# Hymba block, one Trainium2 core: the Gram blocks of the first chunk cut to half width and put first, a smaller first transfer, a final scaling without GpSimd, and a recurrence that begins four matmuls later

## The chip, the cores and the metric

The kernel runs on one core of a Trainium2 chip. The metric is the device time of one execution in microseconds; the median of three runs stands for a kernel. TensorE is called PE here, VectorE DVE, ScalarE ACT, GpSimd POOL and SyncE SP, as in the profile.

## The reference

One layer. A sequence of 512 tokens of width 2048, with 16 learned meta tokens ahead of it, is normalised, projected, sent through a recurrent branch (16 heads of 64, in pairs: 8 pairs) and a gated convolution, mixed, added back and normalised.

```python
hn = _rmsnorm(h_res, norm_in_g[l])                 # (1, 528, 2048)
P  = hn @ w_in[l]                                  # 8 pieces of 1024 columns and a low-rank piece of 128
Pr = Pr + (prev - Pr) * mu_shift[l]                # token shift of r, k, v, g_r and the low-rank columns
decay = exp(-exp(w_raw)); a = sigmoid(a0 + al @ a_lora_up); kk = normalised(k * k_k)
k = k * (1.0 + (a - 1.0) * k_a[l])
# per head, state S of 64x64, over time:
S = S * w_t - (S kk_t) (kk_t*a_t)^T + v_t k_t^T;   y_t = S r_t
y_a = (groupnorm(y) + bonus) * silu(g_r)
y_b = Bg * causal_conv3(Cg * hc) * silu(g_c)
out = _rmsnorm(h_res + concat(y_a, y_b) @ w_out[l], norm_f_g)[:, 16:]
```

## The kernel before

**Projection.** The whole input lies in SBUF as `xh` + `xl`, two parts that add up to the fp32 value, and the weights are split in the same way by `split_w` (L132 to L135, on ACT with DVE or POOL). Each projection therefore takes three matmuls per 128x128 block, hi·hi, hi·lo and lo·hi (`steps`, matmul at L328). `mains` is a generator: it yields one matmul at a time with an estimate of its time, 0.43 ns a column. The projections run in the order of a list `plan`, each into one or two PSUM banks of the pool `pm` with the tag "main"; `scaled` (L352) takes the finished result out of PSUM on DVE.

**Everything else is woven between projection matmuls.** A stage such as `prepare(i)` for head pair i issues its own instructions and then calls `fill(ns)`, which takes as many projection matmuls from `mains` as fill `ns` nanoseconds by the estimate. The table `FW` holds those amounts. So PE's instruction order is written out when the program is built, and a stage on PE always stands between projection matmuls. DVE and ACT are ordered by the scheduler of the tile framework, with `ahead()` (L583) as a raised priority; in some stretches `manual_schedule` keeps the written order.

**Gram blocks.** The sequence is cut into chunks: chunk 0 is the 16 meta tokens in a frame of 64 columns, chunks 1 to 8 hold 64 tokens each (`NCH` is 9). In `prepare(i)` the inner function `gram` (L680) multiplies for each chunk and each of the two heads a 64x128 stationary block of `bk` with a 64x128 moving block of `ar`, in fp32, that is two passes for each matmul. The moving block's first 64 columns are keys, its last 64 columns the receptances `r`; for chunk 0 the latter are zeros. The results go to `za` (chunks 0 to 3, two banks of the tag "tz"), `zc` (chunks 4 to 7, a bank of "misc" and one of "ser") and `ze` (chunk 8, two banks of "main", the tag of the projections). `masked` (L689, instruction at L692) copies them on DVE through the causal mask `gmask` into `gt`, which later transfers read. After the Gram stage `fill(FW["gram2"] ...)` puts projection matmuls, then come the norms `n2` (L714, L715) into "misc" and "tz" and the sum `zb` (L717) into "ser". A bank is written again only when its reader is done, so `za`, `zc` and `ze` each have somebody on PE waiting for their masks.

**Recurrence.** Inverses of the Gram blocks are made for two pairs at a time (`invert`); after the last two, `fill(FW["begin"])` (L929) puts projection matmuls ahead of the recurrence. `load_chunk` brings the operands of a chunk back from DRAM as `ct`, one transfer for each pair; `recur` starts with the matmuls `rz` (L958), four of them for each pair.

**Start.** PE warms up on four passes of a zero tile (`pwarm`, L187). Meanwhile four transfers bring `front`, an array packed by the host: the first (`bt`, 672 columns) has the gain, the first weight block and all 528 columns of `x` tile 0; the second (`r0`, 384 columns) three more weight blocks. `split_x` makes `xh` and `xl` of a tile, and the first projection matmuls (L495, into `ps_lora`) run over both halves of the columns with each operand pair before the next operand pair.

**End.** `finish_last` (L1416) scales the last 128 rows of the output in four pieces of 512 columns by the final norm's factor `r`, on DVE, ACT, POOL and DVE (L1419, L1421, L1423, L1424), and sends each piece off on SP's or ACT's queue.

Of the kernel before, what the change touches and what calls it, by code (L numbers as in the profile page):

```python
# [9 lines left out]
F32 = mybir.dt.float32  # L10
# [34 lines left out]
    tr=3200, lev=3000, cp=4200, out=1500, begin=19500, p=2900, u=2900, s=4800, last=3700, mix=2600,  # L45
# [32 lines left out]
def hymba_kernel(ctx: ExitStack, tc: tile.TileContext, xt, xtok, front, w_in, w_out, pv, lup, cst, msk, gf, out):  # L78
# [126 lines left out]
    def split_x(kt, cols=slice(0, L)):  # L205
        gain = ng[:, kt : kt + 1]
        nc.scalar.activation(xh[:, kt, cols], raw[kt][:, cols], AF.Copy, scale=gain)
        return nc.vector.scalar_tensor_tensor(
            out=xl[:, kt, cols], in0=raw[kt][:, cols], scalar=gain, in1=xh[:, kt, cols].bitcast(F32),
            op0=ALU.mult, op1=ALU.subtract,  # L210
        ).ins

    def square_x(kt, first=False):
        sq = accd if first else tr(f"sqx{kt}")[:, 0:L]
        nc.scalar.activation(sq, raw[kt], AF.Square)
        if not first:
            nc.vector.tensor_tensor(out=accd, in0=accd, in1=sq, op=ALU.add)
# [15 lines left out]
    F0, F1, F2 = KT + P + L, 4 * P + L, 8 * P + 2 * L  # L233
    fr = [view("bt", F0), view("r0", 3 * P), view("bk", F1), view("gt0", F2)]
# [5 lines left out]
    raw[0], raw[1] = fr[0][:, KT + P : F0], fr[2][:, 4 * P : F1]  # L240
# [10 lines left out]
    with tc.manual_schedule(engines={mybir.EngineType.DVE, mybir.EngineType.Activation}):  # L251
        split_piece(0, 0, fr[0][:, KT : KT + P])
        split_x(0, slice(0, L // 2))
        split_x(0, slice(L // 2, L))
        for n in (1, 2, 3):
            split_piece(n, 0, fr[1][:, (n - 1) * P : n * P])
        split_x(1)
        for n in range(4):
            split_piece(n, P, fr[2][:, n * P : (n + 1) * P])
        for kt in (2, 3):  # L260
            split_x(kt)
            if kt == 2:
                for n in range(4):
                    split_piece(n, 2 * P, fr[3][:, 2 * n * P : 2 * (n + 1) * P])
        split_w(1, later_w[0], nc.vector)
        for kt in range(4, 8):
            split_x(kt)
        split_w(3, later_w[1], nc.vector)
        square_x(2, True)
        square_x(3)  # L270
        for n in (2, 3):
            split_w(2 * n + 1, later_w[n], nc.vector)
        square_x(0)
        square_x(1)
        head = split_x(8)
# [207 lines left out]
    def mains():  # L483
# [5 lines left out]
        for k in range(4):  # L489
            for n, (ps, rg) in enumerate(four):  # L490
                if k == n == 0:
                    hi, lo = quarters[0]
                    for ww, xx, first in ((hi, xh, True), (lo, xh, False), (hi, xl, False)):
                        for p, (a, b) in zip(ps, rg):
# [132 lines left out]
    def prepare(i):  # L627
# [51 lines left out]
        gt = cq.tile([P, 2, NCH, P], F32, tag=f"gt{p}", name=f"gt{i}")  # L679
        def gram(z, c, c0):  # L680
            for h, hs, ho in heads:
# [3 lines left out]
                    ar[hs, c].rearrange("p a s -> p (a s)"),  # L685
# [3 lines left out]
        def masked(z, c0, c1):  # L689
            with ahead():  # L690
                for h in range(2):
                    nc.vector.tensor_tensor(  # L692
                        out=gt[:, h, c0:c1],
                        in0=z[h],
                        in1=gmask[:, h].unsqueeze(1).to_broadcast([P, c1 - c0, P]),
# [6 lines left out]
        ze = [pm.tile([P, 1, P], F32, tag="main", name=f"g{i}_8_{h}") for h in range(2)]  # L702
        for c in range(NCH):
            gram((za, zc, ze)[c // 4], c, c // 4 * 4)
        masked(za, 0, 4)
        masked(zc, 4, 8)
        masked(ze, 8, 9)
# [708 lines left out]
    def finish_last(t):  # L1416
# [6 lines left out]
        nc.gpsimd.tensor_scalar(out=here(t, 3), in0=here(t, 3), scalar1=r, scalar2=1.0, op0=ALU.mult, op1=ALU.mult)  # L1423
        nc.vector.tensor_scalar(out=here(t, 1), in0=here(t, 1), scalar1=r, scalar2=1.0, op0=ALU.mult, op1=ALU.mult)  # L1424
        nc.sync.dma_start(o[:, 512:1024], here(t, 1))
        nc.scalar.dma_start(o[:, 1536:DM], here(t, 3))
# [100 lines left out]
```

## Time and profile before

| | us |
|---|---|
| median of the runs | 1001.87 |
| lowest and highest of three runs | 1001.54, 1002.07 |
| the profiled execution's own time | 999.8 |
| its span in the trace | 997.9 |
| PE busy (share of the span) | 986.4 (99%) |
| DVE, ACT, POOL busy | 691.5, 412.7, 268.2 |

The granted clock of the profiled execution is 0.997. PE's busy time is a union of modelled intervals: a matmul's entry begins when its pass begins and ends later than the next one begins, so the distance between two starts is a better measure of what a matmul takes than its own duration. "PEld" is the loading of the stationary operand. A row of the timeline gives the start, the time covered, the engine, the line of the kernel, the instruction, the tile written and the tiles read, how many instructions the row joins, and in brackets the idle time before it with what ended that.

### The profile page before, as it was taken

The page shows a single profiled execution, that of the slowest core. Times are in us where ns is not written, and L with a number is a line of the kernel's source. Part 1 is how long each engine was busy: PE and PEld are TensorE (multiplying, and loading weights), DVE is VectorE, ACT ScalarE, POOL GpSimd, SP SyncE. Part 2 cuts the span into 40 slices and gives each one's busy share as a digit, 9 for nine tenths or more (in the row PEclk, how much of TensorE's full clock was granted, in tenths as well). Part 3 has the DMA queues.
Part 4 walks back from the last instruction along what each step waited for, and adds up shares of the span by engine and source line. Part 5 has one row for each costly group of instructions (what it writes and reads, how often), then busy time and mean ns, then how long its engine had stood idle before and what let it go on. Part 6 is the DMA issues. An engine that isn't in the chain of part 4 may idle for free.

```text
span 997.9 us, 22790 instructions
## 1 busy us (share of the span) xinstructions
PE 986.4 (99%) x9211; PEld 911.0 (91%) x9211; DVE 691.5 (69%) x1314; ACT 412.7 (41%) x770; POOL 268.2 (27%) x286
## 2 busy tenths in 40 slices
PE   9999999999999999999999999999999999999996
PEld 8999999999998999998999998989889898888885
DVE  7687975487765679735579735246555598999895
ACT  7554432353422534232534323233333325645553
POOL 0123323234322324222324222223242422011001
PEclk9999999999999999999999999999999999999998
DMA  9527485437683465854264854988783698698644
GB/s 337 155 70 198 112 218 150 115 105 179 149 226 108 107 178 128 221 148 118 84 180 119 224 142 125 355 259 281 219 262 94 195 260 229 212 297 218 143 102 168
DMA packets 184986, 179.48 MB, mean 180 GB/s; under 512 B 112177, under 2 KB 141617, under 8 KB 184369
## 3 DMA queue, kind: packets, MB, share of 16 engines
q1 hardware_dynamic: 182288, 169.12, 57.9%
q0 software_dynamic: 2304, 8.39, 4.9%
q8 instruction: 72, 1.18, 0.5%
q10 hardware_dynamic: 288, 0.52, 0.1%
q14 instruction: 34, 0.27, 0.1%
HBM read 139.28 MB, written 38.71 MB: 178 GB/s over the span
## 4 chain that ended last, share of the span: by engine, by line
PE 96%; DVE 1%; DMA 1%; issue 1%; POOL 0%; ACT 0%; DVEq 0%; POOLq 0%
PE ps_r L328 9%; PE ps_h L328 9%; PE ps_g L328 9%; PE ps_gc L328 9%; PE ps_B L328 9%; PE ps_v L328 9%; PE ps_C L328 8%; PE ps_k L328 8%; PE M L1243 8%; PE P L1243 4%; PE Q L1243 2%; PE g L682 2%; DMA ct<-opd 1%; PE ps_lora L328 1%; PE rz L958 1%; PE zs L1005 1%
## 5 line engine op out<-in xcount | busy, mean ns | idle before, releaser
L134 ACT CAST w<-wr 128x512 fp32r<-128x512 f32 x252 | 153.4, 619 | 281.0 <-PE ps_h L328 44.7
L135 POOL TENSOR_TENSOR w<-wr,w 128x512 fp32r<-128x512 f32 x119 | 165.8, 1395 | 371.5 <-ACT w L134 331.6
L135 DVE TENSOR_TENSOR w<-wr,w 128x512 fp32r<-128x512 f32 x133 | 99.2, 751 | 99.8 <-ACT w L134 99.6
L328 PE MATMUL ps_r<-xh,w 128*128 128x256 f32 (+1 forms) x512 | 95.2, 282 | 1.0 <-DVE gt L692 1.0
L328 PE MATMUL ps_k<-xh,w 128*128 128x256 f32 (+1 forms) x512 | 95.4, 284 | 0.0
L328 PE MATMUL ps_v<-xh,w 128*128 128x272 f32 (+1 forms) x512 | 95.4, 284 | 0.0
L328 PE MATMUL ps_h<-xh,w 128*128 128x258 f32 (+1 forms) x512 | 93.4, 282 | 0.0
L328 PE MATMUL ps_C<-xh,w 128*128 128x258 f32 (+1 forms) x512 | 93.2, 281 | 0.0
L328 PE MATMUL ps_g<-xh,w 128*128 128x258 f32 (+1 forms) x512 | 91.7, 280 | 0.0
L328 PE MATMUL ps_B<-xh,w 128*128 128x512 f32 x256 | 83.1, 394 | 0.0
L328 PEld LDWEIGHTS ps_r<-xh,w 128*128 128x128 f32 x512 | 80.2, 189 | 1.6 <-DVE gt L692 1.2
L328 PE MATMUL ps_gc<-xh,w 128*128 128x512 f32 x256 | 81.7, 393 | 0.0
L328 PEld LDWEIGHTS ps_k<-xh,w 128*128 128x128 f32 x512 | 80.3, 189 | 0.3
L328 PEld LDWEIGHTS ps_v<-xh,w 128*128 128x128 f32 x512 | 80.1, 189 | 0.3
L328 PEld LDWEIGHTS ps_C<-xh,w 128*128 128x128 f32 x512 | 79.6, 189 | 0.6
L328 PEld LDWEIGHTS ps_h<-xh,w 128*128 128x128 f32 x512 | 79.2, 189 | 0.7
L328 PEld LDWEIGHTS ps_g<-xh,w 128*128 128x128 f32 x512 | 79.2, 189 | 0.2
L328 PE MATMUL ps_k<-xl,w 128*128 128x256 f32 (+1 forms) x256 | 73.0, 285 | 0.0
L328 PE MATMUL ps_v<-xl,w 128*128 128x256 f32 (+1 forms) x256 | 72.5, 283 | 0.0
L328 PE MATMUL ps_g<-xl,w 128*128 128x256 f32 (+1 forms) x256 | 72.4, 283 | 0.0
L328 PE MATMUL ps_r<-xl,w 128*128 128x256 f32 (+1 forms) x256 | 72.1, 282 | 0.0
L328 PE MATMUL ps_C<-xl,w 128*128 128x256 f32 (+1 forms) x256 | 71.9, 281 | 0.0
(312 smaller groups left out, 2205.8 us busy)
## 6 DMA issues: line engine op xcount, KB each, us to landing
wr<-in_w_in_dram SPq DMA_DIRECT2D x126, 512.0 KB
ct<-opd SPq DMA_DIRECT2D x56, 320.0 KB
wo<-in_w_out_dram SPq DMA_DIRECT2D x21, 512.0 KB
opd<-gt SPq DMA_DIRECT2D x16, 576.0 KB
x<-in_w_out_dram POOLq DMA_DIRECT2D x16, 512.0 KB, 5.7
opd<-ar SPq DMA_DIRECT2D x8, 576.0 KB
opd<-bt SPq DMA_DIRECT2D x64, 64.0 KB
ct<-opd SPq DMA_DIRECT2D x16, 256.0 KB
```

Of the source, the lines that this page charges most:

```text
L134: nc.scalar.copy(hi, rq)
L135: low[q] = eng.tensor_tensor(out=lo, in0=rq, in1=hi.bitcast(F32), op=ALU.subtract).ins
L328: nc.tensor.matmul(ps[r], ww[:, w], xx[:, kt, a:b], start=(kt == 0 and n == 0), stop=(kt == KT - 1 and n == 2))
L682: nc.tensor.matmul(z[h][:, c - c0], bk[hs, c, h : h + 2, :].rearrange("p a s -> p (a s)"), ar[hs, c].rearrange("p a s -> p (a s)"), start= ...
L958: nc.tensor.matmul(z[e][ho if e else hs, 0, k], ct[e][hs, k, o : o + CH], uv(e, k, hs, h) if part else st[hs, 4 * e + k], start=(part == 0 ...
L1005: nc.tensor.matmul(zs[hs, j], bb[:, h], uv(e, k, everything, h), start=True, stop=True)
L1243: nc.tensor.matmul(bank[s], left(prod, jj, m, s), w, start=(jj == 0 and n == 0), stop=(jj == 7 and n == 2))
```

## The change

Four edits that have nothing to do with each other.

1. `gram` takes only the first 64 columns of `ar` as moving operand where the chunk is 0. Chunk 0 now goes to `ze`, which shrinks to 64 columns and is computed first and masked first; `za` holds chunks 1 to 4 and `zc` chunks 5 to 8. The upper half of `gt` for chunk 0 is now set to zero by a POOL memset.
2. The first transfer holds only the first 256 columns of `x` tile 0 (400 columns in all) and goes to `r0`; the other 272 go with the second transfer (656 columns) to `bt`. The first weight block's high part is made on DVE, not on ACT. The first matmuls finish the first half of the columns before the second half.
3. `finish_last` gives the piece that POOL scaled to DVE (192 columns) and ACT (320 columns).
4. `FW["begin"]` goes from 19500 to 19900.

```diff
@@ -42,7 +42,7 @@
 
 FW = dict(
     evac=34, start=1062, lora=2200, gram=8000, gram_b=13500, gram2=5500, misc=2000, v=2000, vt=1000, solve=24500, solve_first=30000,
-    tr=3200, lev=3000, cp=4200, out=1500, begin=19500, p=2900, u=2900, s=4800, last=3700, mix=2600,
+    tr=3200, lev=3000, cp=4200, out=1500, begin=19900, p=2900, u=2900, s=4800, last=3700, mix=2600,
 )
 
 
@@ -202,17 +202,17 @@
         for k in range(n):
             raw[a + k] = t[:, k * L : (k + 1) * L]
 
-    def split_x(kt, cols=slice(0, L)):
-        gain = ng[:, kt : kt + 1]
-        nc.scalar.activation(xh[:, kt, cols], raw[kt][:, cols], AF.Copy, scale=gain)
+    def split_x(kt):
+        gain, h = ng[:, kt : kt + 1], xh[:, kt, 0:L]
+        nc.scalar.activation(h, raw[kt], AF.Copy, scale=gain)
         return nc.vector.scalar_tensor_tensor(
-            out=xl[:, kt, cols], in0=raw[kt][:, cols], scalar=gain, in1=xh[:, kt, cols].bitcast(F32),
-            op0=ALU.mult, op1=ALU.subtract,
+            out=xl[:, kt, 0:L], in0=raw[kt], scalar=gain, in1=h.bitcast(F32), op0=ALU.mult, op1=ALU.subtract
         ).ins
 
     def square_x(kt, first=False):
         sq = accd if first else tr(f"sqx{kt}")[:, 0:L]
-        nc.scalar.activation(sq, raw[kt], AF.Square)
+        for cols, t in ((slice(0, L), raw[kt]),) if kt else x0:
+            nc.scalar.activation(sq[:, cols], t, AF.Square)
         if not first:
             nc.vector.tensor_tensor(out=accd, in0=accd, in1=sq, op=ALU.add)
 
@@ -230,14 +230,16 @@
 
     for n in range(4):
         quarters[2 * n] = slot_of(2 * n)
-    F0, F1, F2 = KT + P + L, 4 * P + L, 8 * P + 2 * L
-    fr = [view("bt", F0), view("r0", 3 * P), view("bk", F1), view("gt0", F2)]
+    X0 = L - SEQ // 2
+    F0, F1, F2 = KT + P + SEQ // 2, 4 * P + L, 8 * P + 2 * L
+    fr = [view("r0", F0), view("bt", X0 + 3 * P), view("bk", F1), view("gt0", F2)]
     o = 0
     for t in fr:
         nc.sync.dma_start(t, front[:, o : o + t.shape[1]])
         o += t.shape[1]
     ng = fr[0]
-    raw[0], raw[1] = fr[0][:, KT + P : F0], fr[2][:, 4 * P : F1]
+    x0 = ((slice(0, SEQ // 2), fr[0][:, KT + P : F0]), (slice(SEQ // 2, L), fr[1][:, 0:X0]))
+    raw[1] = fr[2][:, 4 * P : F1]
     for k in range(2):
         raw[2 + k] = fr[3][:, 8 * P + k * L : 8 * P + (k + 1) * L]
     later_w = [load_w(0, "g")]
@@ -249,11 +251,18 @@
     load_x("vs", 11, 1)
     nc.sync.dma_start(pvt, pv)
     with tc.manual_schedule(engines={mybir.EngineType.DVE, mybir.EngineType.Activation}):
-        split_piece(0, 0, fr[0][:, KT : KT + P])
-        split_x(0, slice(0, L // 2))
-        split_x(0, slice(L // 2, L))
+        hi, lo = (t[:, 0:P] for t in quarters[0])
+        w0 = fr[0][:, KT : KT + P]
+        nc.vector.tensor_copy(hi, w0)
+        nc.vector.tensor_tensor(out=lo, in0=w0, in1=hi.bitcast(F32), op=ALU.subtract)
+        for cols, t in x0:
+            nc.scalar.activation(xh[:, 0, cols], t, AF.Copy, scale=ng[:, 0:1])
+            nc.vector.scalar_tensor_tensor(
+                out=xl[:, 0, cols], in0=t, scalar=ng[:, 0:1], in1=xh[:, 0, cols].bitcast(F32),
+                op0=ALU.mult, op1=ALU.subtract,
+            )
         for n in (1, 2, 3):
-            split_piece(n, 0, fr[1][:, (n - 1) * P : n * P])
+            split_piece(n, 0, fr[1][:, X0 + (n - 1) * P : X0 + n * P])
         split_x(1)
         for n in range(4):
             split_piece(n, P, fr[2][:, n * P : (n + 1) * P])
@@ -490,8 +499,8 @@
             for n, (ps, rg) in enumerate(four):
                 if k == n == 0:
                     hi, lo = quarters[0]
-                    for ww, xx, first in ((hi, xh, True), (lo, xh, False), (hi, xl, False)):
-                        for p, (a, b) in zip(ps, rg):
+                    for p, (a, b) in zip(ps, rg):
+                        for ww, xx, first in ((hi, xh, True), (lo, xh, False), (hi, xl, False)):
                             nc.tensor.matmul(p, ww[:, 0:P], xx[:, 0, a:b], start=first, stop=False)
                             yield (b - a) * 0.43
                     continue
@@ -677,34 +686,37 @@
         fill(FW["gram_b" if p else "gram"] + shift)
 
         gt = cq.tile([P, 2, NCH, P], F32, tag=f"gt{p}", name=f"gt{i}")
+        nc.gpsimd.memset(gt[:, :, 0, CH:P], 0.0)
+
         def gram(z, c, c0):
             for h, hs, ho in heads:
                 nc.tensor.matmul(
                     z[h][:, c - c0],
                     bk[hs, c, h : h + 2, :].rearrange("p a s -> p (a s)"),
-                    ar[hs, c].rearrange("p a s -> p (a s)"),
+                    ar[hs, c].rearrange("p a s -> p (a s)") if c else ar[hs, c, 0],
                     start=True, stop=True,
                 )
 
-        def masked(z, c0, c1):
+        def masked(z, c0, c1, n=P):
             with ahead():
                 for h in range(2):
                     nc.vector.tensor_tensor(
-                        out=gt[:, h, c0:c1],
+                        out=gt[:, h, c0:c1, 0:n],
                         in0=z[h],
-                        in1=gmask[:, h].unsqueeze(1).to_broadcast([P, c1 - c0, P]),
+                        in1=gmask[:, h, 0:n].unsqueeze(1).to_broadcast([P, c1 - c0, n]),
                         op=ALU.mult,
                     )
 
 
         za = [pz.tile([P, 4, P], F32, tag="tz", name=f"g{i}_0_{h}") for h in range(2)]
         zc = [pi.tile([P, 4, P], F32, tag=("misc", "ser")[h], name=f"g{i}_4_{h}") for h in range(2)]
-        ze = [pm.tile([P, 1, P], F32, tag="main", name=f"g{i}_8_{h}") for h in range(2)]
-        for c in range(NCH):
-            gram((za, zc, ze)[c // 4], c, c // 4 * 4)
-        masked(za, 0, 4)
-        masked(zc, 4, 8)
-        masked(ze, 8, 9)
+        ze = [pm.tile([P, 1, CH], F32, tag="main", name=f"g{i}_8_{h}") for h in range(2)]
+        gram(ze, 0, 0)
+        for c in range(1, NCH):
+            gram((za, zc)[c // 5], c, 1 + c // 5 * 4)
+        masked(ze, 0, 1, CH)
+        masked(za, 1, 5)
+        masked(zc, 5, 9)
         fill(FW["gram2"] - shift + 1300 * (i == 1) + 2000 * (i == 3))
 
         n2 = tr(f"n2{i}")
@@ -1420,9 +1432,11 @@
         nc.sync.dma_start(o[:, 1024:1536], here(t, 2))
         nc.scalar.activation(here(t, 0), here(t, 0), AF.Copy, scale=r)
         nc.scalar.dma_start(o[:, 0:512], here(t, 0))
-        nc.gpsimd.tensor_scalar(out=here(t, 3), in0=here(t, 3), scalar1=r, scalar2=1.0, op0=ALU.mult, op1=ALU.mult)
         nc.vector.tensor_scalar(out=here(t, 1), in0=here(t, 1), scalar1=r, scalar2=1.0, op0=ALU.mult, op1=ALU.mult)
         nc.sync.dma_start(o[:, 512:1024], here(t, 1))
+        a, b = here(t, 3)[:, 0:192], here(t, 3)[:, 192:512]
+        nc.scalar.activation(b, b, AF.Copy, scale=r)
+        nc.vector.tensor_scalar(out=a, in0=a, scalar1=r, scalar2=1.0, op0=ALU.mult, op1=ALU.mult)
         nc.scalar.dma_start(o[:, 1536:DM], here(t, 3))
 
     with tc.manual_schedule(engines={mybir.EngineType.DVE, mybir.EngineType.Activation, mybir.EngineType.Pool}):
```

Line numbers move by 9 to 14 from L328 on: L328 becomes L337, L352 becomes L361, L682 becomes L693, L692 becomes L703, L958 becomes L970.

Three places of the instruction order follow. The first is PE at the Gram stage of pair 0, in the first stretch of projections: `ps_r_0` is a projection matmul, `g_0`, `g_4` and `g_8` are the banks `za`, `zc` and `ze`, with the head as the next number. Before:

```order
L328 MATMUL ps_r_0_1098<-xh,w_826 128x256
L682 MATMUL g_0_0_1136<-ar_755,bk_756 128x128
L682 MATMUL g_0_1_1137<-ar_755,bk_756 128x128
L682 MATMUL g_0_0_1136<-ar_755,bk_756 128x128
L682 MATMUL g_0_1_1137<-ar_755,bk_756 128x128
...
L682 MATMUL g_4_0_1138<-ar_755,bk_756 128x128
L682 MATMUL g_4_1_1139<-ar_755,bk_756 128x128
L682 MATMUL g_8_0_1140<-ar_755,bk_756 128x128
L682 MATMUL g_8_1_1141<-ar_755,bk_756 128x128
L328 MATMUL ps_r_0_1098<-xh,w_826 128x256
```

Now:

```order
L337 MATMUL ps_r_0_1099<-xh,w_827 128x256
L693 MATMUL g_8_0_1142<-ar_756,bk_757 128x64
L693 MATMUL g_8_1_1143<-ar_756,bk_757 128x64
L693 MATMUL g_0_0_1138<-ar_756,bk_757 128x128
L693 MATMUL g_0_1_1139<-ar_756,bk_757 128x128
L693 MATMUL g_0_0_1138<-ar_756,bk_757 128x128
...
L693 MATMUL g_4_0_1140<-ar_756,bk_757 128x128
L693 MATMUL g_4_1_1141<-ar_756,bk_757 128x128
L337 MATMUL ps_r_0_1099<-xh,w_827 128x256
```

The two matmuls into `g_8` have moved from the end of the stage to its start and are 64 columns wide. The projection matmuls around the stage are the same.

The second place is DVE at the masks of pair 2 (`gt` is the masks' output, `pr_k` the next projection's copy out of PSUM, `w` a weight split). Before:

```order
L822 STREAM_TRANSPOSE vs_3136<-v_2781 128x576
L135 TENSOR_TENSOR w_2858<-wr_2856,w_2858 128x512
L692 TENSOR_TENSOR gt_2919<-g_0_0_2920,cs 128x512
L692 TENSOR_TENSOR gt_2919<-g_0_1_2921,cs 128x512
L692 TENSOR_TENSOR gt_2919<-g_4_0_2922,cs 128x512
L692 TENSOR_TENSOR gt_2919<-g_8_0_2924,cs 128x128
L692 TENSOR_TENSOR gt_2919<-g_4_1_2923,cs 128x512
L692 TENSOR_TENSOR gt_2919<-g_8_1_2925,cs 128x128
L352 TENSOR_TENSOR pr_k_2969<-ps_k_0_2801,rs 128x256
L352 TENSOR_TENSOR pr_k_2969<-ps_k_1_2802,rs 128x256
```

Now:

```order
L834 STREAM_TRANSPOSE vs_3140<-v_2784 128x576
L135 TENSOR_TENSOR w_2861<-wr_2859,w_2861 128x512
L703 TENSOR_TENSOR gt_2922<-g_8_0_2928,cs 128x64
L703 TENSOR_TENSOR gt_2922<-g_8_1_2929,cs 128x64
L703 TENSOR_TENSOR gt_2922<-g_0_0_2924,cs 128x512
L703 TENSOR_TENSOR gt_2922<-g_0_1_2925,cs 128x512
L703 TENSOR_TENSOR gt_2922<-g_4_0_2926,cs 128x512
L703 TENSOR_TENSOR gt_2922<-g_4_1_2927,cs 128x512
L361 TENSOR_TENSOR pr_k_2973<-ps_k_0_2804,rs 128x256
L361 TENSOR_TENSOR pr_k_2973<-ps_k_1_2805,rs 128x256
```

The two masks of `g_8` stood fourth and sixth of the six and now stand first and second; the weight split `w` is still ahead of all of them.

The third place is PE ahead of the first `rz`, where the recurrence begins (`ps_C` and `ps_h` are projections). Before:

```order
L328 MATMUL ps_C_1_8171<-xl,w_8050 128x258
L328 MATMUL ps_C_1_8171<-xh,w_8050 128x258
L328 MATMUL ps_h_0_8289<-xh,w_8110 128x256
L328 MATMUL ps_h_0_8289<-xl,w_8110 128x256
L328 MATMUL ps_h_0_8289<-xh,w_8110 128x256 x2
L328 MATMUL ps_h_0_8289<-xl,w_8110 128x256
L328 MATMUL ps_h_0_8289<-xh,w_8110 128x256 x2
L328 MATMUL ps_h_0_8289<-xl,w_8110 128x256
L958 MATMUL rz_0_8323<-ct_0_8303 64x64 x2
L958 MATMUL rz_1_8324<-ct_0_8304 64x64 x2
```

Now:

```order
L337 MATMUL ps_C_1_8180<-xl,w_8059 128x258
L337 MATMUL ps_C_1_8180<-xh,w_8059 128x258
L337 MATMUL ps_h_0_8298<-xh,w_8119 128x256
L337 MATMUL ps_h_0_8298<-xl,w_8119 128x256
L337 MATMUL ps_h_0_8298<-xh,w_8119 128x256 x2
L337 MATMUL ps_h_0_8298<-xl,w_8119 128x256
L337 MATMUL ps_h_0_8298<-xh,w_8119 128x256 x2
L337 MATMUL ps_h_0_8298<-xl,w_8119 128x256
L337 MATMUL ps_h_0_8298<-xh,w_8119 128x256 x2
L337 MATMUL ps_h_0_8298<-xl,w_8119 128x256
L337 MATMUL ps_h_0_8298<-xh,w_8119 128x256
L970 MATMUL rz_0_8336<-ct_0_8316 64x64 x2
```

Four more matmuls of `ps_h` stand ahead of the first `rz`, twelve where eight stood.

## The prediction

> **What bounds the kernel now.** I read the page first, for the engine that is full and the chain that ended last.
>
> ```profile
> span 997.9 us, 22790 instructions
> PE 986.4 (99%) x9211; PEld 911.0 (91%) x9211; DVE 691.5 (69%) x1314; ACT 412.7 (41%) x770; POOL 268.2 (27%) x286
> PE 96%; DVE 1%; DMA 1%; issue 1%; POOL 0%; ACT 0%; DVEq 0%; POOLq 0%
> ```
>
> PE is busy nearly throughout and carries 96% of the chain. So an edit can gain in two ways only: a PE instruction goes or becomes shorter, or one of PE's few waits goes. The view of waits, for PE, lists them:
>
> ```profile
> PE pwarm L187 <- DVE cold L184: 1.4, 1, 1.4
> PE ps_r L328 <- DVE gt L692: 1.0, 1, 1.0
> PE rz L958 <- DMA ct<-opd: 0.5, 2, 0.3
> PE rz L979 <- issue: 0.4, 1, 0.4
> ```
>
> The change points at two of these, a projection that waits for masks (1.0) and the first `rz` (0.5). The rest of the span, 986 of 998 us, is work that it touches only in 16 of 144 Gram matmuls. The whole prize is small.
>
> **Masks of `ze` first (pair 2).** The timeline of PE around the longer wait:
>
> ```profile
> 217.67 0.28 PE L328 MATMUL ps_k<-xl,w 128*128 128x272 f32 x1
> 217.80 0.29 PE L328 MATMUL ps_k<-xh,w 128*128 128x272 f32 x1
> 219.04 0.38 PE L328 MATMUL ps_r<-xh,w 128*128 128x256 f32 x1 [0.96 <-DVE gt L692]
> 219.26 0.28 PE L328 MATMUL ps_r<-xl,w 128*128 128x256 f32 x1
> ```
>
> Two steps of the chain in that stretch:
>
> ```profile
> 217.00 2.01 DVE gt L692 x4
> 219.00 0.04 issue
> ```
>
> The new projection `ps_r` needs a bank of `ze`, and four masks run from 217.00 to 219.00 before it is free. A projection pass normally starts 0.13 after the one before (217.67 to 217.80). Here 1.24 passes, and the next takes 0.22 instead of about 0.12 (the pace of `ps_h` below): 1.11 + 0.10 = 1.21 us lost. In the new order both masks of `ze` come first and are narrower than the 128x128 ones; two short operations from 217.00 on end before PE reaches 217.93, where `ps_r` would start without a wait. At the mean of the four masks (2.01 / 4 = 0.50) they would end at 218.00, and 0.1 would stay. I take the whole 1.21. `za` and `zc` come free later by what the two short masks take, but their next writers on PE, the norms, stand behind the further projection matmuls of `fill(FW["gram2"])`. Nothing else is late there.
>
> **Gram blocks of chunk 0 at 64 columns.** The rows of the loads of the stationary operand, and one of a 64-column kind:
>
> ```profile
> 45.28 0.76 PEld L460 LDWEIGHTS pss<-cs,accd 128*128 128x128 f32 x6
> 80.61 2.09 PEld L682 LDWEIGHTS g<-ar,bk 64*128 64x128 f32 x36
> 638.22 1.18 PE L1005 MATMUL zs<-ct 128*64 128x64 f32 x32
> ```
>
> The 36 passes of a Gram stage run two at a time, one for each head: 18 steps in 2.09 with one load of 0.19, (2.09 - 0.19) / 17 = 0.112 each. The loads of `pss` belong to matmuls with 128 stationary columns and, by the code, a single moving one, and they follow each other at (0.76 - 0.19) / 5 = 0.114. So 128 moving columns or one, the step is the same: the load of 128 stationary columns paces it, and `bk` keeps its 128. I take 0. The other end is the `zs` row, with 64 columns on both sides: 16 steps of two in 1.18, about (1.18 - 0.22) / 15 = 0.064. If the moving side set the pace, 8 pairs x 2 passes x (0.112 - 0.064) = 0.77 us would go.
> The Trainium skill, "TensorE: Matmul & The Clock Gate", section "Back-to-back issue gap", counts a pass by its moving columns, 134 cycles at 128 and about 60 at up to 64; by it alone the narrow blocks would gain. Its section "LDWEIGHTS (loading the stationary operand)" gives the columns of the stationary operand divided by 1.2 ns, 107 ns here and unchanged, and the 0.112 and 0.114 of this trace agree with that one.
>
> **`ze` at the head of the stage: an earlier need for its bank.** In before `ze` was written at the end of the stage, almost 2 us after it began; now it is its first instruction. It takes the two "main" banks of the projection that finished before, which must have been copied out by DVE. The rows where that comes nearest:
>
> ```profile
> 79.82 0.89 DVE L352 TENSOR_TENSOR pr_k<-ps_k,rs 128x256 f32<-128x256 f32 x4
> 80.61 2.28 PE L682 MATMUL g<-ar,bk 64*128 64x128 f32 x36
> 121.71 0.45 DVE L352 TENSOR_TENSOR pr_g<-ps_g,rs 128x256 f32<-128x256 f32 x2
> 122.33 0.38 PE L682 MATMUL g<-ar,bk 64*128 64x128 f32 x2
> 544.15 0.56 DVE L352 TENSOR_TENSOR pr_v<-ps_v,rs 128x256 f32<-128x256 f32 x3
> 545.16 0.38 PE L682 MATMUL g<-ar,bk 64*128 64x128 f32 x2
> ```
>
> At pair 0 the copy ends at 80.71 and the stage begins at 80.61; with 0.04 from a DVE end to a PE start (the row at 219.00) that is a new wait of 0.14. At pair 1 the copy ends at 122.16, 0.17 ahead of the stage: no wait, by a hair. At pair 7 it has 0.45. Cost 0.14. Behind a late `ze` stands the whole stage and all of PE, since PE takes its instructions in order.
>
> **Pair 1's `zb`.** One more place where the masks' order acts, in the timelines of DVE and of PE:
>
> ```profile
> 125.71 1.60 DVE L135 TENSOR_TENSOR w<-wr,w 128x512 fp32r<-128x512 f32 x1
> 127.24 2.87 DVE L692 TENSOR_TENSOR gt<-g,cs 128x512 f32<-128x512 f32 x6
> 130.03 0.68 DVE L135 TENSOR_TENSOR w<-wr,w 128x512 fp32r<-128x512 f32 x1
> ```
>
> ```profile
> 129.63 0.29 PE L715 MATMUL n_tz<-sq_l,ones 128*2 128x288 f32 x1
> 130.05 0.47 PE L717 MATMUL zb<-rk_h,ones 128*128 128x512 f32 x1
> ```
>
> `zb` starts 0.42 after the pass before it, 0.29 more than usual, because the masks of `zc` end late. They are now last of six, but the six are shorter in sum; I put them 0.06 later, and PE arrives 0.14 later from pair 0. The wait shrinks by 0.08; its bounds are +0.1 and -0.29, the whole of it.
>
> **`begin` 400 ns later.** PE at the first `rz`:
>
> ```profile
> 629.13 0.58 PE L958 MATMUL rz<-ct 64*64 64x64 f32 x24
> 629.87 0.33 PE L958 MATMUL rz<-ct 64*64 64x64 f32 x4 [0.17 <-DMA ct<-opd]
> 630.55 0.33 PE L958 MATMUL rz<-ct 64*64 64x64 f32 x4 [0.35 <-DMA ct<-opd]
> ```
>
> And the pace of `ps_h` a little later:
>
> ```profile
> 637.78 0.40 PE L328 MATMUL ps_h<-xh,w 128*128 128x256 f32 x2
> 638.01 0.28 PE L328 MATMUL ps_h<-xl,w 128*128 128x258 f32 x1
> ```
>
> The last two groups of four wait for their pairs' transfers, 0.17 and 0.35 of shown idle time. An emptied pipeline costs more than the idle that is shown: at 217.80 it was 1.11 for 0.96, so 0.15 more. Two of them make 0.52 + 0.30 = 0.82 us. The four matmuls now ahead of `rz` take (638.01 - 637.78) / 2 = 0.115 each, 0.46 in all. They are work that has to be done anyway, so as long as the transfers land when they did, 0.46 of the 0.82 is filled and 0.36 stays. The transfers are issued by SP, whose order there is the same but for one other load. Bounds: 0, if the transfers move back with PE; 0.82, if they land a little earlier.
>
> **Start.** PE's and ACT's first rows:
>
> ```profile
> 1.45 3.78 PE L187 MATMUL pwarm<-cold 128*128 128x512 f32 x4 [1.45 <-DVE cold L184]
> 4.60 1.41 PE L495 MATMUL ps_lora<-xh,w 128*128 128x256 f32 x4
> 4.86 0.68 ACT L227 CAST w<-in_r 128x128 fp32r<-128x128 f32 x3
> ```
>
> The first projection pass is entered at 4.60, while the warm-up passes still run (to 5.23): a transfer that lands sooner finds PE occupied. The second transfer's data was in use at 4.86 and stays at about that place, as the two together have the same 1056 columns; the second half of `x` is now in it, and PE comes to it only after three passes of the first half. Cost 0, between -0.1 and +0.3 (the cast of three blocks, 0.68, now stands behind that half on ACT).
>
> **End.** The last scalings and their sends:
>
> ```profile
> 992.51 0.92 DVE L1424 TENSOR_SCALAR xa<-xa,fv 128x512 f32<-128x512 f32 x1
> 993.33 0.40 ACTq L1426 DMA_DIRECT2D out_dram<-xb  x1
> 993.46 0.33 SPq L1425 DMA_DIRECT2D out_dram<-xa  x1
> ```
>
> The stretches behind them (busy times of the engines, the clock, the DMA engines' share, GB/s):
>
> ```profile
> 993.50:996.00 2.50, 0.00 (x0) 0.00 (x0) 0.00 (x0) 0.00 (x0) 0.00 (x0) 0.50 1.02 379
> 996.00:996.50 0.50, 0.00 (x0) 0.00 (x0) 0.00 (x0) 0.00 (x0) 0.00 (x0) 0.50 0.49 172
> ```
>
> From 993.50 on no engine works; the DMA engines are full (share 1.02) until about 996.2. DVE's piece, slowed to 0.92 beside POOL, should go out near 993.0, while the piece shared by DVE and ACT goes out near 993.8, 0.5 later than now. The queue is full meanwhile, so the end stays: 0, with 0.3 to either side.
>
> POOL's new memsets, one for each pair, stand beside others that wait for the same tiles, with POOL busy for 27%: 0, with up to 0.1 on either side.
>
> **The sum.** -1.21 - 0.46 + 0.14 - 0.08 = -1.61. The profiled execution took 999.8, so 998.2 in its terms; it lies 2.07 below the median, so on the scale of the runs 1001.87 - 1.61 = 1000.3. The bounds of the unknown terms (begin -0.36 to +0.46, end and start 0.3 each, `zb` -0.29 + 0.08 to +0.1 + 0.08) mostly cancel: 999.5 to 1001.2 for this case. A measurement of this kernel can tell 0.2%, 2.0 us, from no change: faster means under 999.87, slower over 1003.87. The forecast falls short of that bound by a little.
>
> **Rivals.**
> - *The moving side paces the Gram stage.* -0.77 more, with the bounds as above: 999.5, faster. For it speaks the `zs` row, against it the `pss` row. Chance 0.10.
> - *The copy out of PSUM becomes the bound (slower).* `ze` now needs DVE at pairs 0 and 1 with no room. If the scheduler's shuffled DVE order puts slow weight splits in front of the copy there, PE stops. One such split took 1.60 where the next took 0.68, 0.92 more. Two in front of each copy: 1.84 at pair 0 and 1.84 - 0.13 = 1.71 at pair 1, 3.55 in all, and `zb` keeps its 0.08: 1003.9. It begins at a slip of 0.13 at pair 1 and has eaten the gain at about 0.8 at each. For it: margins of -0.14 and +0.13. Against it: in before DVE copies both without a wait that PE shows. Chance 0.11, with smaller slips in it.
> - *The mask wait only moves.* `ps_r` is let through and the next reader of a bank, or the recurrence's transfers, wait instead, so most of the two gains goes: about 1001.5, the same. PE in order and DVE late at 217 speak for it, the projection matmuls that stand between `ps_r` and the norms against it. Chance 0.12.
>
> **How the numbers follow.** The main case has 0.67; its lower third or so lies under 999.87, where the rest of the `rz` wait or the 0.4 of issue at L979 also goes. Faster: 0.67 x 0.36 + 0.10 = 0.34. Slower: 0.11 (its smaller slips stay within the bound, and the tail of the main case makes up for them). Same: 0.55. The range of 8 in 10 leaves out the slow rival's upper part and the combinations with everything gained: 998.9 to 1002.4.
>
> **What would show it.** In the trace of after: no wait of `ps_r` for masks near 217; the first `rz` wait shorter by about 0.46; the Gram loads at the same 0.112, some 2.09 for 36; a short wait of the first Gram matmul of pair 0 for `pr_k`; the same full DMA after the last scaling. I am wrong if that first Gram matmul waits over 0.5 at any pair, if a Gram stage is shorter by 0.1, or if the stretch before the first projections or after the last matmul differs by over 0.3.

## The result, and the profile after

| | before | changed |
|---|---|---|
| median of 21 runs each, us | 1001.25 | 1002.84 |
| lowest and highest | 999.99, 1002.22 | 1001.31, 1004.62 |
| profiled execution: span in the trace | 997.9 | 1001.6 |

The ratio is 1.0015, with a 95% interval of 1.0010 to 1.0021: the change costs 1.0 to 2.1 us. I had forecast 1.6 us less than before; 1002.84 lies above the range, which ended at 1002.4. The profiled execution of before (999.8) is faster than any of its 21 runs listed here, so the 3.7 us between the two spans overstate the difference.

The longest waits of PE in the changed kernel:

```profile
PE g L693 <- DVE pr_g L361: 1.5, 2, 1.2
PE pwarm L187 <- DVE cold L184: 1.4, 1, 1.4
PE ps_lora L337 <- ACT w L227: 1.4, 1, 1.4
PE rz L991 <- issue: 0.3, 1, 0.3
PE ps_lora L337 <- DVE xl L208: 0.2, 1, 0.2
PE rz L970 <- DMA ct<-opd: 0.2, 1, 0.2
```

The wait of `ps_r` for masks is gone and the first `rz` waits 0.2 where it waited 0.5. Two of over 1 us are new: the Gram stage waits for `pr_g`, the copy of a projection out of PSUM, and the projection `ps_lora` waits near the start.

**Pair 1.** PE's timeline at the Gram stage, and DVE's ahead of it:

```profile
124.54 0.43 PE L693 MATMUL g<-ar,bk 64*128 64x64 f32 x2 [0.23 <-DVE pr_g L361]
126.22 3.02 PE L693 MATMUL g<-ar,bk 64*128 64x64 f32 x34 [1.25 <-DVE pr_g L361]
```

```profile
124.07 0.42 DVE L361 TENSOR_TENSOR pr_g<-ps_g,rs 128x256 f32<-128x256 f32 x1
124.40 1.30 DVE L742 STREAM_TRANSPOSE bt<-bk 128x512 f32<-128x512 f32 x2
125.62 0.45 DVE L361 TENSOR_TENSOR pr_g<-ps_g,rs 128x256 f32<-128x256 f32 x2
```

The first bank that `ze` needs is copied out from 124.07, the rest, behind two transposes, from 125.62 to 126.07. Each releases one of the two `ze` matmuls: 0.23 + 1.25 = 1.48 us of shown waiting in all. In before the last copy ended at 122.16; it is 3.9 later, while PE's Gram stage is only 2.2 later. The rest of the Gram stage, 34 passes, runs for 3.02, where all 36 took 2.28 in before. The windows of 3.4 us around the wait and behind it (PE, PEld, DVE, ACT and POOL busy; then the granted clock, the DMA share and GB/s) say why. The granted clock is the share of PE's full clock that its throttle lets through.

```profile
124.00:127.40 3.40, 1.92 (x25) 1.62 (x25) 2.61 (x7) 0.72 (x1) 1.27 (x1) 1.00 0.34 76
127.45:130.85 3.40, 3.40 (x26) 3.18 (x23) 2.70 (x4) 1.66 (x3) 1.46 (x3) 0.51 0.24 81
```

PE is busy 1.92 of 3.4 us in the first, and in the second the granted clock is at 0.51. In steps of 0.05 us, the low clock adds up to 3.41 us at half speed, 1.71 us lost.

**Why DVE is late there.** Of pair 1's preparation, the step `te` and POOL's `ta` that waits for it, before (L648, L652) and changed (L657, L661):

```profile
108.38 0.75 DVE L648 SCALAR_TENSOR_TENSOR te<-ta,e 128x576 f32<-128x576 f32 x1
109.24 1.67 POOL L652 TENSOR_SCALAR ta<-ta,hv 128x576 f32<-128x576 f32 x1 [4.28 <-DVE te L648]
```

```profile
114.22 0.74 DVE L657 SCALAR_TENSOR_TENSOR te<-ta,e 128x576 f32<-128x576 f32 x1
115.08 1.45 POOL L661 TENSOR_SCALAR ta<-ta,hv 128x576 f32<-128x576 f32 x1 [5.55 <-DVE te L657]
```

`te` is 5.84 us later. The scheduler has put it behind the steps of pair 0's inverse and the copies of `pr_v`. Everything that follows from POOL's `ta` moves with it, and the copies of `pr_g` stand behind those steps in DVE's order. The DVE instructions up to `pr_g`'s second copy are the same but for one cast more at the start; their order is not.

**Start.** ACT's first use of the third transfer, `in_bk`, which the change does not touch, before and changed:

```profile
5.88 0.74 ACT L207 ACTIVATE xh<-in_bk,in_bt 128x528 fp32r<-128x528 f32 x1 [0.33 <-DMA in_bk<-in_front_dram]
```

```profile
8.30 0.73 ACT L207 ACTIVATE xh<-in_bk,in_r 128x528 fp32r<-128x528 f32 x1 [2.98 <-DMA in_bk<-in_front_dram]
```

The first transfer came earlier and PE reached `ps_k` at 5.56 instead of 6.11; then it waited for the third, whose last packet ended at 7.94 instead of 5.51.

### The profile page after: what moved, and what is told of

It is laid out like the page before. It is cut to its first block, busy times and chain, and to the rows that moved or that the text cites. A ratio compares the mean times of both kernels' runs of the same rounds, so it can differ in the third digit from the quotient of the medians.

```text
span 1001.6 us, 22805 instructions
## 1 busy us (share of the span) xinstructions
PE 988.3 (99%) x9211; PEld 912.7 (91%) x9211; DVE 690.4 (69%) x1316; ACT 412.5 (41%) x771; POOL 270.9 (27%) x293
## 4 chain that ended last, share of the span: by engine, by line
PE 93%; DMA 2%; DVE 2%; issue 2%; POOL 1%; ACT 0%; SPq 0%; POOLq 0%; ACTq 0%; DVEq 0%
PE ps_k L337 9%; PE ps_r L337 9%; PE ps_h L337 9%; PE ps_B L337 9%; PE ps_v L337 9%; PE ps_gc L337 8%; PE ps_C L337 8%; PE M L1255 8%; PE ps_g L337 7%; PE P L1255 4%; PE Q L1255 2%; PE g L693 2%; PE ps_lora L337 1%; PE rz L970 1%; PE zs L1017 1%
## 5 line engine op out<-in xcount | busy, mean ns | idle before, releaser
L135 DVE TENSOR_TENSOR w<-wr,w 128x512 fp32r<-128x512 f32 x133 | 96.8, 734 | 94.9 <-ACT w L134 94.5
L337 PE MATMUL ps_k<-xh,w 128*128 128x256 f32 (+1 forms) x512 | 95.4, 284 | 0.0
L337 PE MATMUL ps_v<-xh,w 128*128 128x272 f32 (+1 forms) x512 | 95.4, 283 | 0.0
L337 PE MATMUL ps_r<-xh,w 128*128 128x256 f32 (+1 forms) x512 | 95.2, 282 | 0.0
L337 PE MATMUL ps_h<-xh,w 128*128 128x258 f32 (+1 forms) x512 | 94.3, 282 | 0.0
L337 PE MATMUL ps_g<-xh,w 128*128 128x258 f32 (+1 forms) x512 | 92.4, 281 | 0.0
L337 PE MATMUL ps_C<-xh,w 128*128 128x258 f32 (+1 forms) x512 | 91.9, 280 | 0.0
L337 PE MATMUL ps_B<-xh,w 128*128 128x512 f32 x256 | 83.1, 394 | 0.0
L337 PE MATMUL ps_gc<-xh,w 128*128 128x512 f32 x256 | 81.6, 393 | 0.0
L337 PEld LDWEIGHTS ps_r<-xh,w 128*128 128x128 f32 x512 | 80.3, 190 | 0.4
L337 PEld LDWEIGHTS ps_h<-xh,w 128*128 128x128 f32 x512 | 79.9, 189 | 0.7
L337 PEld LDWEIGHTS ps_k<-xh,w 128*128 128x128 f32 x512 | 80.2, 189 | 0.3
L337 PEld LDWEIGHTS ps_v<-xh,w 128*128 128x128 f32 x512 | 80.1, 189 | 0.3
L337 PEld LDWEIGHTS ps_g<-xh,w 128*128 128x128 f32 x512 | 79.8, 191 | 0.2
L337 PEld LDWEIGHTS ps_C<-xh,w 128*128 128x128 f32 x512 | 79.2, 189 | 0.2
L337 PE MATMUL ps_k<-xl,w 128*128 128x256 f32 (+1 forms) x256 | 73.0, 285 | 0.0
L337 PE MATMUL ps_g<-xl,w 128*128 128x256 f32 (+1 forms) x256 | 72.9, 285 | 0.0
L337 PE MATMUL ps_C<-xl,w 128*128 128x256 f32 (+1 forms) x256 | 72.6, 284 | 0.0
L337 PE MATMUL ps_v<-xl,w 128*128 128x256 f32 (+1 forms) x256 | 72.5, 283 | 0.0
L337 PE MATMUL ps_r<-xl,w 128*128 128x256 f32 (+1 forms) x256 | 72.1, 282 | 0.0
```

What stands on the lines that cost most here:

```text
L135: low[q] = eng.tensor_tensor(out=lo, in0=rq, in1=hi.bitcast(F32), op=ALU.subtract).ins
L337: nc.tensor.matmul(ps[r], ww[:, w], xx[:, kt, a:b], start=(kt == 0 and n == 0), stop=(kt == KT - 1 and n == 2))
```

## The experiments

The time of each is compared with the kernel before on the same chip, as a ratio with its 95% interval; with eight to eleven runs of a kernel the interval is some 1 us to either side. The three kernels with added waits ran once each, for their traces (1013.24, 1012.54 and 1037.37 us).

**One part at a time.** First the Gram edit alone, in the kernel before (its hunk of the diff).

> The kernel before with the Gram edit alone; start, end and begin as before. Theory P (pair 1): the Gram edit makes the first Gram matmul of pair 1 wait for the copy of pr_g, over 1 us, because DVE reaches that copy some 2 us later (the order of DVE there is that of the changed kernel) and because ze is now needed at once; a drop of the granted clock to 0.5 for some 3 us follows. It costs about 3.3 us, and 1.1 us come back at pair 2: 2 us slower than before. Theory S (start): the loss is the third transfer of the start, which this kernel has as before: 1 us faster than before.

1003.68 us, ratio 1.0024 (1.0015 to 1.0033). Its waits:

```profile
PE g L684 <- DVE pr_g L352: 1.5, 2, 1.2
...
PE rz L961 <- DMA ct<-opd: 0.5, 2, 0.3
```

The wait of 1.48 and 3.41 us at half clock are here with the old start: the Gram edit alone makes the loss at pair 1. Then all the rest without it.

> The changed kernel with its Gram edit undone: new start, new end, begin 19900. Theory P: no wait at pair 1, the mask wait of 1.0 at pair 2 stays, the first rz waits 0.2 to 0.4 less, the projections begin 0.5 earlier at the start: faster than before by 0.5 to 1 us. Theory S: the third transfer lands at 8.3 instead of 5.9 again and PE waits 1.4 near 8: slower than before by 1 to 1.5 us.

1000.72 us, ratio 0.9995 (0.9986 to 1.0004), no wait and no low clock at pair 1, `ps_r` waits 0.9. The rest alone makes no loss that these runs can tell.

**The early bank or DVE's order?** The Gram edit does two things at pair 1: it needs `ze`'s bank sooner, and it comes with another order of DVE. This kernel takes the early need away and keeps the order:

```diff
-        gram(ze, 0, 0)
+        if i != 1:
+            gram(ze, 0, 0)
         for c in range(1, NCH): ...
+        if i == 1:
+            gram(ze, 0, 0)
```

> The changed kernel, but for pair 1 alone the two matmuls of chunk 0 stand at the end of the Gram stage again; the order of DVE is the same. Theory P: DVE is as late as in the changed kernel, but the bank is needed some 2 us later, so the wait at pair 1 is under 0.3, the clock stays at 1.0, and it is about 3 us faster than the changed kernel, 1 to 2 us faster than before. Theory S: no more than 0.5 faster than the changed kernel.

1002.44 us, ratio 1.0015 (1.0005 to 1.0024). My theory P, a late DVE that is felt because the bank is needed at once, had promised under 0.3 of wait; there was more, further on:

```profile
130.45 0.40 PE L337 MATMUL ps_g<-xh,w 128*128 128x258 f32 x2
132.51 0.29 PE L729 MATMUL n_misc<-sq_h,ones 128*2 128x288 f32 x1 [1.66 <-DVE gt L703]
```

DVE's order is that of the changed kernel. The Gram stage passed, and the norms waited 1.66 for a mask instead, with the same 3.41 us of low clock behind it. So the early need only decides which instruction meets a DVE that is late in any case. Two theories were left for the next run: D, that DVE's new order is the cause, and E, that the early need is. The order changes with the place of the two matmuls at pair 0: with `ze` last at pair 0 alone (the same edit with `i > 0`), DVE's order at pair 1 is that of before, while `ze` still stands first at pair 1.

> The changed kernel with the two matmuls of chunk 0 at the end of the Gram stage for pair 0 alone; at pairs 1 to 7 they stand first. The order of DVE at pair 1 is that of before. Theory D: pr_g is copied out in time, the first Gram matmul of pair 1 waits 0 to 0.2, the clock stays at 1.0, as fast as the kernel with chunk 0 last everywhere. Theory E: pair 1 still waits over 1 us and runs 3 us at half clock, about as slow as the changed kernel.

1000.69 us, ratio 0.9996 (0.9987 to 1.0005). The Gram stage of pair 1 does not wait at all and the clock stays at 1.0. D holds and E falls. The direct test leaves PE's order alone and raises the priority of one DVE instruction; behind it a few steps on DVE (`ta`, a weight split, `sq_l`, a transpose) change places too:

```diff
-        nc.vector.scalar_tensor_tensor(out=te, in0=ta, scalar=1.0, in1=e2, op0=ALU.add, op1=ALU.mult)
+        with ahead() if i == 1 else nullcontext():
+            nc.vector.scalar_tensor_tensor(out=te, in0=ta, scalar=1.0, in1=e2, op0=ALU.add, op1=ALU.mult)
```

> The changed kernel with one DVE instruction of pair 1 (te, which POOL and then DVE wait for) at raised priority, so that it stands ahead of the inverse's steps and the copies of pr_v again; PE's order is that of the changed kernel. Theory D (DVE's order at pair 1): pr_g is copied some 2 us earlier, the first Gram matmul of pair 1 waits under 0.3, the clock stays at 1.0, 2.5 to 3.5 us faster than the changed kernel, 0 to 1 us faster than before. Theory E (the early need alone): still a wait over 1 us and the low clock.

999.45 us, ratio 0.9984 (0.9975 to 0.9992). `te` starts at 109.24, and the Gram stage runs through:

```profile
109.24 0.75 DVE L658 SCALAR_TENSOR_TENSOR te<-ta,e 128x576 f32<-128x576 f32 x1
...
122.35 0.45 DVE L361 TENSOR_TENSOR pr_g<-ps_g,rs 128x256 f32<-128x256 f32 x2
```

```profile
123.43 2.28 PE L694 MATMUL g<-ar,bk 64*128 64x64 f32 x36
```

One instruction at raised priority turns a loss of 0.15% into a gain of 0.16%. With that, DVE's order is shown to be the cause of the wait; what makes the low clock behind it is taken up below.

**Masks first.** Two kernels asked what the masks' order is worth by itself: one with `ze` last for all pairs but masked first, and the kernel before with nothing but `masked(ze, ...)` moved ahead of the other two calls.

> The changed kernel with the two matmuls of chunk 0 at the end of the Gram stage for all pairs; narrow, masked first, start, end and begin as changed. The order of DVE at pair 1 is that of before. Both theories, D (DVE's new order at pair 1 is the cause) and E (the early need of ze's bank is): no wait over 0.3 at pair 1, no low clock, the wait at pair 2 gone (-1.2), begin -0.2 to -0.4, start between -0.5 and +0.9: 0.5 to 2 us faster than before. If the start costs what its three profiles show (+0.9), no more than 0.7 faster.

> The kernel before with one thing changed: the masks of ze stand first of the six, with the chunks, widths and the order on PE as before. Both theories: the wait of ps_r at pair 2 (0.96 shown) goes or falls under 0.2, nothing else moves: 1.0 to 1.3 us faster than before.

They took 1000.25 us (ratio 0.9990, 0.9981 to 0.9999) and 1001.42 us (1.0002, 0.9993 to 1.0011), and in both `ps_r` waits as before, against what I expected:

```profile
PE ps_r L337 <- DVE gt L703: 0.9, 1, 0.9
```

```profile
PE ps_r L328 <- DVE gt L692: 0.9, 1, 0.9
```

DVE's masks stand in the old order in both, `g_0`, `g_0`, `g_4`, `g_8`, `g_4`, `g_8`: here they follow the order in which PE computes the blocks, and the order of the calls changes nothing. Only with PE computing `ze` first do its masks stand ahead, so the gain at pair 2 comes from the move on PE. The second kernel, with DVE's masks and PE's order those of before, also serves as a second profile of before, with a span of 999.5.

**The start.** Undone in the changed kernel (its four hunks), and alone in the kernel before.

> The changed kernel with the start of before (first transfer of 672 columns). Theory P: the wait at pair 1 and the low clock stay, some 3 us; it is within 0.7 of the changed kernel. Theory S: no wait near 8 us, 1.5 to 2 us faster than the changed kernel and at or below before.

> The kernel before with the new start alone. Theory L (the start is a loss): the third transfer lands after 7.3, PE waits near 8 or works through slower, the sums of squares (prs) come 0.7 to 1.2 later than in the kernels with the old start (49.4 to 50.3), and the time is 0.7 to 1.2 us above before. Rival: prs at 49.5 to 50.3 and the time within 0.4 of before.

Undone: 1003.20 us, 1.0018 (1.0009 to 1.0027), no gain that shows against 1.0015. Alone: 1002.09 us, 1.0011 (1.0002 to 1.0020), a loss. The traces of all kernels tell more: ACT first uses the third transfer at 5.88 to 7.44 in the nine traces with the old start and at 7.45 to 8.42 in the seven with the new one, 1.2 later in the mean; the matmuls `prs`, which end this stretch, start at 49.4 to 50.3 (mean 50.0) and at 50.3 to 51.3 (mean 50.9). The new start costs about 0.9 us by these. Half of the packets of the third transfer take 0.161 us or less in every trace; 17 to 31 of its 128 took over 0.25 in the seven traces with the new start (23 in the changed kernel), 3 to 13 in the nine with the old one (9 in before). What slows them was not tried and is left open.

**The versions that follow.** The Gram edit with `ze` last at pair 0, `begin` 19900, old start and end:

> The kernel before with the Gram edit (at pair 0 the two matmuls of chunk 0 stay at the end) and begin 19900; start and end as before. Theory D with the start as a loss of about 1 us: pair 2's wait gone (-1.2), begin -0.5: 1.3 to 2 us faster than before and the fastest of all. If the start costs nothing: as fast as the kernel that differs from this in start and end (0.3 faster than before).

999.60 us, ratio 0.9988 (0.9979 to 0.9997); the faster of the two promised values, 1.3 below before. Then the Gram edit whole, with `te` ahead at pair 1, `begin` 19900, old start and end:

> The kernel before with the Gram edit as changed, te of pair 1 at raised priority, and begin 19900; start and end as before. If the start's loss and the cure at pair 1 add up: 0.7 to 1.2 us faster than the changed kernel with the cure alone, some 2 to 2.5 us faster than before. If the start's loss is an effect of single executions: within 0.4 of the changed kernel with the cure.

998.80 us where before took 1001.70, ratio 0.9976 (0.9965 to 0.9986): 1.4 to 3.5 us faster than before, and by the ratios faster than the changed kernel too. Its interval overlaps that of the kernel with the new start and `te` ahead (0.9975 to 0.9992), so it does not show what the old start adds. In its profile one wait of PE is left in the view of waits:

```profile
PE pwarm L187 <- DVE cold L184: 1.4, 1, 1.4
```

**What lowers the clock.** Three kernels leave PE idle at set places, two between projections and one ahead of Gram stages, by round trips of PE and DVE. In outline:

```diff
+            nc.tensor.matmul(zw, cs[:, C_ID : C_ID + P], stall[:, 0:CH], start=True, stop=True)
+            nc.vector.tensor_copy(stall[:, 0:CH], zw)      # then further DVE instructions on stall
+            nc.tensor.matmul(zw_e, cs[:, C_ID : C_ID + P], stall[:, 0:CH], start=True, stop=True)
```

> The kernel before with one to four round trips PE to DVE to PE added after the zb stage of pairs 2 to 7 (1, 2, 3, 4, 2, 3 of them), to leave PE idle for different times; their results are used by nothing else. Clock by idle time: stretches of over about 1.3 us idle within some 3 us are followed within 3 us by some 3 us at a granted clock of 0.5, stretches under 1 us by none. Rival, clock by what happens at pair 1 alone: no low clock after any of them.

> The kernel before with one round trip PE to DVE to PE at each of the pairs 2 to 7, lengthened by further DVE instructions so that PE idles once at each for about 0.9, 1.1, 1.3, 1.5, 1.8 and 2.1 us; the results are used by nothing else. Clock by idle time: the granted clock falls to 0.5 for some 3 us after the longer ones and stays at 1.0 after those up to 1.0; the edge lies between 1.0 and 1.5. Rival: none falls, and the low clock at pair 1 has another cause.

> The kernel before with one round trip PE to DVE to PE of about 1.6 us idle right ahead of the Gram stage of each of the pairs 2 to 7, results unused. If the low use of the array in the Gram stage counts with the wait: a granted clock of 0.5 for 3.4 us behind most of the six. If the length of the wait and its place against a window of fixed period alone count: behind few or none of them, as behind the waits of 1.57 to 1.76 between projections.

The short ones (up to four of 0.32 in 3 us) left the clock at 1.0. So did single waits of 1.04, 1.11, 1.24, 1.57, 1.70 and, the longest of them, this:

```profile
229.47 0.43 PE L734 MATMUL zw_e<-stall,cs 128*128 128x64 f32 x2 [1.76 <-DVE stall L732]
```

I had expected a low clock behind the longer ones. Ahead of the Gram stages the waits came out much longer than meant, 3.4 to 4.6 us; five of the six were followed by a low clock, and one of them, ahead of pair 5's, was not:

```profile
419.67 0.43 PE L688 MATMUL zw_e<-stall,cs 128*128 128x64 f32 x2 [3.39 <-DVE stall L686]
```

The 3.4 us behind it, at a clock of 1.00:

```profile
419.60:423.00 3.40, 3.33 (x44) 3.14 (x45) 1.79 (x4) 0.00 (x0) 0.53 (x1) 1.00 0.77 143
```

So the length of a wait does not decide alone: 1.48 to 1.66 at pair 1 were followed by a low clock in the profiled execution of each of the four kernels with that wait, and 3.39 at pair 5 was not. The place of a wait counts too. In the clock records of all sixteen traces, every fall comes a whole number of 3.413 us after the trace's first record of the full clock: 36 of them in the changed kernel (4.61 to 127.49), 35 to 37 in the other three, 62, 78, 106, 153 and 168 in the run with the long waits. So I count by these windows. Two of the changed kernel, each with the one behind it:

```profile
8.02:11.44 3.42, 1.93 (x13) 1.72 (x14) 1.58 (x5) 2.17 (x7) 0.00 (x0) 1.00 0.95 335
11.44:14.85 3.41, 3.41 (x28) 3.27 (x27) 3.28 (x7) 2.96 (x8) 0.00 (x0) 1.00 0.99 369
124.08:127.49 3.41, 1.93 (x27) 1.63 (x27) 2.62 (x7) 0.72 (x1) 1.22 (x1) 1.00 0.37 83
127.49:130.90 3.41, 3.41 (x25) 3.19 (x22) 2.71 (x4) 1.66 (x3) 1.51 (x3) 0.50 0.21 77
```

The first and the third left PE idle for 1.49 and 1.48 us alike; behind the one the clock stayed at 1.00, behind the other it was 0.50. And the two between which the wait of 3.39 was split:

```profile
414.68:418.09 3.41, 1.60 (x14) 1.46 (x13) 2.47 (x9) 1.35 (x2) 1.44 (x2) 1.00 0.66 177
418.09:421.51 3.42, 1.84 (x28) 1.77 (x30) 1.77 (x5) 0.00 (x0) 0.53 (x1) 1.00 0.99 238
```

That wait left PE idle for 1.81 and 1.58 us of its windows; the other five of the run left 1.98 to 2.76 in one. In all sixteen traces, the stretch after the last matmul included, each of the 21 windows at full clock with 1.96 us of idle PE or more was followed by a fall, and none with less than 1.48. Of the eight between, four were (1.48, 1.48, 1.50 and 1.80, all at pair 1) and four were not (1.49, 1.58, 1.66 and 1.81). What decides there is not shown; whether the matmuls that stand beside the wait count is open.

The low stretches at pair 1 each lasted one such window, those of the run with the long waits two. The Trainium skill, "TensorE: Matmul & The Clock Gate" (Part 1), has a window of 3.41 us that runs freely and does not begin with the kernel; the length of the low stretches and the distances of the falls agree with it. Its rule that the clock falls after an idle window of some 3.4 us does not agree with the falls ahead of the last matmul, behind windows that were idle for 1.48 to 2.76.

The low clock need not come in every execution. The mean granted clock of each, which the idle end lowers too, is 0.995 or 0.996 in 8 of the 21 executions of the changed kernel, in 7, 3 and 3 of the 11 of the other three with the wait, and never under 0.997 in the 97 listed of before or the 85 of the kernels without it. The 1.71 us make 0.0017 of the span, so some executions of the four probably went without the low clock; the profiled one of the changed kernel (0.996) had it.

## Why the prediction was wrong, point by point

**`ze` at the head of the stage: the step that failed.** I read the margin at pair 1 (the copy ends 0.17 ahead of the stage) from the trace of before and carried it over as if DVE would reach the copy at the same time. The change had moved DVE's order there, and the copy came 3.9 us later. My sign of being wrong, a Gram matmul that waits over 0.5, came true with 1.25, on the second one of pair 1. The rival "the copy out of PSUM becomes the bound", with a chance of 0.11, had the place and the wait, but a different cause: slow weight splits in front of the copies at pairs 0 and 1. The splits there took 0.65 and 0.69, not 1.60, so it is luck that its price of 3.55 came near the size. From the start of pair 0's Gram stage to that of pair 2 the changed kernel takes 136.75 us, and the kernel with `te` ahead 133.49. The 3.26 between them are the 1.48 of wait, the 1.71 of low clock and 0.07 more. The half clock was in none of my cases. At pair 0 I had 0.14; the stage and what follows to `zb` lost 0.19.

**Masks at pair 2: right.** -1.21 forecast; from pair 2's Gram stage to pair 3's the changed kernel takes 1.2 less than before, with both masks of `ze` first on DVE. What I had not asked is what puts them first: PE computing `ze` first, not the order of the calls.

**Pair 1's `zb`: too small.** -0.08 forecast. `zb` starts 0.13 after the pass before it in the changed kernel, where PE comes late, and also in the kernel with `te` ahead, so all of the 0.29 is gone. That is inside the bounds.

**Narrow blocks: right.** Pair 5's stationary loads, before and changed:

```profile
396.11 2.09 PEld L682 LDWEIGHTS g<-ar,bk 64*128 64x128 f32 x36
```

```profile
400.39 2.09 PEld L693 LDWEIGHTS g<-ar,bk 64*128 64x128 f32 x36
```

Half the moving columns in 4 of the 36 passes change nothing; the rival with 0.77 falls.

**`begin`: not contradicted.** -0.46 forecast. From pair 7's Gram stage to PE's last matmul start, four traces with 19500 take 444.6 to 444.8 us, nine with 19900 take 443.1 to 445.1, 443.9 in the mean: -0.7, but the nine alone spread over 2.0. The waits at `rz` are 0.5 to 0.7 with 19500 and 0 to 0.7 with 19900.

**Start: wrong.** 0 forecast, with +0.3 at most; about +0.9 by the traces, and 0.2 to 2.0 by the times of the new start alone. I followed the first two transfers and took the third, of equal size and place in the queue, as given.

**End: right.** From PE's last matmul start to the span's end it is 8.19 in before and 8.29 in the changed kernel: 0.1 lost, inside the 0.3. The memsets on POOL were not measured by themselves.

The parts, each from where it was measured by itself, add up to 2.4 (Gram edit alone) + 0.9 - 0.7 + 0.1 = 2.7, against 1.0 to 2.1 for the whole. The intervals of the parts cover the gap; that they do not quite add, with the start's loss hidden behind pair 1's, is not excluded. With `te` ahead, and so without the step that failed, the kernel is 0.8 to 2.5 us faster than before. The forecast of 1.61 lies in that, in part by luck, as the start's term and `zb`'s are off in opposite directions.

## What to carry to other kernels

Where a scheduler orders an engine, an edit on another engine moves its instructions too: compare that order around every wait with little room before carrying a margin from the old trace to the new kernel. When a wait appears, ask why the engine it waits for is late, not only why it is needed so soon: taking the early need away moved this wait to the next reader, and one priority on one instruction removed it. A wait on a full TensorE may cost twice its length, if the clock falls behind it: here 1.48 us of wait brought 1.71 us of lost clock.

## What the runs showed that I had not expected

- Waits of 1.48 to 1.66 us on PE were followed by 3.41 us at a granted clock of 0.5 in the profiled executions of four kernels (1.71 us lost each time), while waits of 1.70, 1.76 and 3.39 us elsewhere were not. Every fall lies on a grid of 3.413 us, and the 3.39 were split between two windows of it.
- A transfer whose own bytes, queue place and home were untouched was first used 1.2 us later in the mean when the two transfers ahead of it were cut differently, with 17 to 31 of its packets over 0.25 us instead of 3 to 13.
